# The end of the attention in a diffusion layer: one tile's output rows earlier, another's half moved, four roundings on another engine

## The chip, the cores and the metric

One NeuronCore of a Trainium2 chip runs one layer of a diffusion backbone. The metric is the device time of one execution in microseconds; smaller is better. Five engines work side by side, each through its own list of instructions in the order in which it was written, and they wait for each other by semaphores: PE (TensorE, matmuls), DVE (VectorE), ACT (ScalarE), POOL (GpSimd) and SP (SyncE, which issues the transfers).

## The reference

```python
def rmsnorm(x, g):
    xf = x.astype(jnp.float32)
    y = xf * lax.rsqrt(jnp.mean(xf * xf, axis=-1, keepdims=True) + EPS)
    return (y * g.astype(jnp.float32)).astype(x.dtype)
# window_attention: 8 query heads, 2 kv heads of 64; keys with |i-j| <= 128, 256 context keys, a sink logit
    p = jax.nn.softmax(jnp.concatenate([s_band, s_ctx, s_sink], axis=-1), axis=-1).astype(v.dtype)
    out = (jnp.einsum('bnhgqk,bnkhd->bnqhgd', p[..., :n_band], vb)
           + jnp.einsum('bnhgqc,bchd->bnqhgd', p[..., n_band:n_band + k_ctx.shape[1]], v_ctx))
def conv_glu(h, w_up, conv_w, conv_b, w_down):
    a, val = jnp.split(h @ w_up, 2, axis=-1)
    a = jax.nn.gelu(dwconv(a, conv_w, conv_b))
    return (a * val) @ w_down
```

The layer takes 1024 latent tokens of width 1024: the norm, an adaLN shift and scale, one input projection for an mLSTM group (4 heads of 128) and the window attention, both results side by side (512 + 512 columns) through one output projection `w_out`, gated and added to `x`; then the norm, shift and scale again and the ConvGLU (`D_FF` 2816), gated and added.

`rmsnorm(x)` is `x * rsqrt(mean(x * x) + EPS)`. All is float32 from outside.

## The kernel before

**Number format.** A float32 operand of a matmul is split into a rounded part (`hi`, written as `F32R`) and the rest (`lo = src - hi`), and a product is three matmuls: hi x hi, lo x hi, hi x lo (`mm3`, lines 305 to 307). The rounding is a copy with a change of type (CAST in the profile); it can be done on ACT or on DVE. The subtraction for `lo` is DVE's here (line 1210), and it reads what the rounding wrote.

**The window attention** goes over 32 pairs in stages `t` = 0 to 33, inside a `manual_schedule`: the code's order is each engine's order. In one stage the pair `N` starts, `A` has its scores and softmax, `C` transposes its probabilities (`tr`), splits them (`hi`, `lo`) and multiplies by the values (`pv`), and `E` finishes (`y1`, `y2` on DVE empty the product's bank `u`; its pool has one buffer). Between these steps stand slots: `fill(t, i)` runs what the dictionary `more[t, i]` holds. There the output projection of earlier tiles is spread: class `Wout` has `load` (the tile's rows `x2`), `hi` and `lo`, `mm(n, kt)` (one step of three matmuls; four steps make half `n` of a tile, 512 columns, in the bank `po`) and `add(n)` (DVE adds the bank to the rows; after `n` = 1 they are stored). `f0` is the attention part of tile 0; `tail_of(f0, n - 2)` puts its eight steps into stages 31, 32 and 33 (`n` = 32).

**The end of attention** is a loop over the other seven tiles in the order 4, 1, 5, 2, 6, 3, 7, inside a second `manual_schedule`. Iteration `i` with tile `b`: PE projects half 0 of the tile's attention rows (`wout_n(b, 0)`, 12 matmuls); ACT squares the second half of the tile before and takes the root (`sq(prev, 1)`); `norm_b(prev)` has DVE's reciprocal and ACT's scaling into `hn`; `evac(pp)` empties the transposes of the tile two before into `raw`, four pieces on ACT and four on DVE; DVE adds half 0 to the rows (`add0`); ACT squares it (`sq(b, 0)`); then the splits and sums that the FFN needs from tile `pp`; then PE projects half 1 (`wout_n(b, 1)`), transposes `prev` (`trans`), and DVE adds half 1 (`add1`). The projection banks of the loop, `pO2`, are two. `held` is a list of subtractions that `run` lets DVE do later.

In iterations 1, 3 and 5, `pp` is tile 0, 1 and 2, whose `raw` (128 x 1024) is split into the FFN's operand B11, with DVE for both parts; in iteration 0 DVE rounds `er`, a tile of FFN weights, into `e0`:

```python
V.tensor_copy(e0[0][:], er[:])
held.append(split(pp, B11, 2, raws[pp][:], V))
```

Ahead of the loop ACT squares tile 0's two halves into `hn` (`sq(0, 0)`, `sq(0, 1)`), takes the root (with a load of ACT's function table), and `norm_b(0)` follows. Behind the loop comes the FFN: long sequences of matmuls on `hB` (the split operands) and weights from `w_up`, then `w_down`. The FFN takes over half of the time.

Lines are those of the kernel before; the kernel after has the same code 27 to 29 lines further down.

Of the kernel before, what the change touches and what calls it, by code (L numbers as in the profile page):

```python
# [9 lines left out]
F32 = mybir.dt.float32  # L10
F32R = mybir.dt.float32r
BF16 = mybir.dt.bfloat16
AF = mybir.ActivationFunctionType
ALU = mybir.AluOpType
# [4 lines left out]
P = 128  # L19
D = 1024  # L20
# [14 lines left out]
EPS = 1e-6  # L35
BIG = 1e30
XW = 272
PB = 6
# [40 lines left out]
def build(tc, I, out, dbg=None):  # L79
    nc = tc.nc  # L80
    dbg = dbg or {}
    V, S, G, T = nc.vector, nc.scalar, nc.gpsimd, nc.tensor
# [13 lines left out]
    def spc(n, i=0, w=1):  # L96
        a = SP[n][0] + i
        return sp[:, a:a + w]
# [186 lines left out]
    hn = [0]  # L285
# [197 lines left out]
    m0, me = z, e_  # L483
    order = (list(range(NCH)), [1, 0] + list(range(NCH - 1, NC - 1, -1)))
# [450 lines left out]
    def load_q(b):  # L935
        QTs[b] = wm.tile([P, AH, P], F32R, name="QT", tag="QT", bufs=2)
        return nc.sync.dma_start(QTs[b][:].bitcast(F32), q_d[b]).ins
# [38 lines left out]
    n = 0  # L976
# [12 lines left out]
    for h in range(H):  # L989
# [3 lines left out]
        else:  # L993
# [12 lines left out]
            pq = rstk.enter_context(tc.tile_pool(name="pq", bufs=1, side="right"))  # L1006
# [60 lines left out]
    xs = {}  # L1067
# [140 lines left out]
    order = [4, 1, 5, 2, 6, 3, 7]  # L1208
    ys = {}
# [23 lines left out]
    more = collections.defaultdict(list)  # L1233
# [7 lines left out]
    def tail_of(w, t):  # L1241
        m = lambda n, k: lambda: w.mm(n, k)
        more[t + 1, 1] += [m(0, 0)]
        more[t + 1, 2] += [m(0, 1)]
        more[t + 2, 0] += [m(0, 2)]
        more[t + 2, 1] += [m(0, 3), lambda: w.add(0)]
        more[t + 3, 0] += [m(1, 0)]
        more[t + 3, 1] += [m(1, 1)]
        more[t + 3, 2] += [m(1, 2), m(1, 3), lambda: w.add(1)]

    def fill(t, i):
        for f_ in more.pop((t, i), ()):
            f_()

    w0, f0 = Wout(0, 0), Wout(0, 1)
# [4 lines left out]
    for b in range(1, NL):  # L1260
        token(Wout(b, 0), 4 * b - 2)
    n = len(pairs)
    more[n - 4, 0] += [f0.load]
    more[n - 3, 2] += [f0.hi, f0.lo]
    tail_of(f0, n - 2)
    more[n - 5, 0] += [lambda: ysplit_h(order[0], S)]
    more[n - 5, 2] += [lambda: ysplit_l(order[0])]
    more[n - 4, 0] += [lambda: ysplit_h(order[1], S)]
# [20 lines left out]
    for t in range(n + 2):  # L1289
        blk, nth = divmod(t, 4)  # L1290
        if nth == 0 and blk + 1 < NL:
            lq = load_q(blk + 1)
        if t in WOT:
            k = 4 + WOT.index(t)
            room = [wop.tile([P, D], F32R, name=f"wo{n}{k}")[:] for n in "hl"]
            with tc.issue_after(lq):
                wogs.append(load_wo(k, lambda room=room: room, G, True))
                next(wogs[-1])
        if t + 1 < len(pairs):
            live[t + 1] = Pair(*pairs[t + 1])  # L1300
        N, A, B, C, E = (live.get(t + 1 - i, null) for i in range(5))
        A.S(0)
        E.lo(2)
        B.nrm()
        fill(t, 3)
        rows_step()
        if t == 0:
            next(qpend.pop(0), 0)
            w0.tr()
            pdk.close()  # L1310
            pSs.append((pa_.enter_context(tc.tile_pool(name="pS", bufs=1, space=PSUM, side="right")), "s"))
            live[0].sk(1)
            w0.hi()
            live[0].S(1)
            w0.lo()
        E.pv(1)
        C.tr(0)
        E.pv(2)
        A.mxo(0)
        C.hi(0)  # L1320
        E.y1()
        A.ex(0)
        N.sk(0)
        C.lo(0)
        E.y2()
        fill(t, 0)
        if t == 0:
            for q in qpend:
                next(q, 0)
        C.tr(1)  # L1330
        if t:
            A.S(1)
        C.hi(1)
        A.mxo(1)
        fill(t, 1)
        C.tr(2)
        C.lo(1)
        A.ex(1)
        N.sk(1)
        C.hi(2)  # L1340
        fill(t, 2)
        C.pv(0)
        live.pop(t - 3, None)
# [19 lines left out]
    t5 = pb_.enter_context(tc.tile_pool(name="t5", bufs=2, reuse_waits="tile"))  # L1363
# [5 lines left out]
    B11, B21, B22, T1, T2, T3, T4 = range(7)  # L1369
# [5 lines left out]
    er = eW.tile([P, 2, 512], F32, name="er")  # L1375
    e0 = [eW.tile([P, 2, 512], F32R, name=f"e0{n}") for n in "hl"]
# [12 lines left out]
    hns, rs, pts, raws, tbs = ({} for _ in range(5))  # L1389
    last = order[-1]  # L1390

    def load_x(b):
        xs[b] = t3.tile([P, D], F32, name="x2", tag="x2")[:]
        nc.sync.dma_start(xs[b], x2_d[b][:])

    def wout_n(b, n, mid=None):
        ns = slice(512 * n, 512 * n + 512)
        po = pO.tile([P, 512], F32, name="po", tag="o")
        yh, yl = ys[b]
        for kt in range(4):  # L1400
            if kt == 3 and mid:
                mid()
            mm3(po[:], yh[:, kt], yl[:, kt], wos[4 + kt][0][:, ns], wos[4 + kt][1][:, ns], kt == 0, kt == 3)
        return lambda: V.tensor_tensor(out=xs[b][:, ns], in0=po[:], in1=xs[b][:, ns], op=ALU.add)
# [4 lines left out]
    def sq(b, n, mean=True):  # L1409
        if n == 0:  # L1410
            hns[b] = t5.tile([P, D], F32, name="hn", tag="hn")
            rs[b] = t5.tile([P, 3], F32, name="r2", tag="r2")
        ns = slice(512 * n, 512 * n + 512)
        S.activation(hns[b][:, ns], xs[b][:, ns], AF.Square, accum_out=rs[b][:, n:n + 1])
        if n == 1:
            if mean:
                run(1)
                mean0(b)
            S.activation(rs[b][:, 0:1], rs[b][:, 1:2], AF.Sqrt, bias=rs[b][:, 2:3], scale=1.0 / D)

    def norm_b(b, halves=False):
        run(1)
        V.reciprocal(rs[b][:, 0:1], rs[b][:, 0:1])
        if halves:
            S.activation(hns[b][:, 0:512], xs[b][:, 0:512], AF.Copy, scale=rs[b][:, 0:1])
            V.tensor_scalar(out=hns[b][:, 512:D], in0=xs[b][:, 512:D], scalar1=rs[b][:, 0:1], scalar2=None, op0=ALU.mult)
        else:
            S.activation(hns[b][:], xs[b], AF.Copy, scale=rs[b][:, 0:1])
# [26 lines left out]
    held = []  # L1455
# [5 lines left out]
    def split(b, blk, w, src, hi_eng=S):  # L1461
        ts = slice(b % 4 * P, b % 4 * P + P)
        hi, lo = (hB[i][:, blk:blk + w, :, ts] for i in range(2))
        (S.copy if hi_eng is S else hi_eng.tensor_copy)(hi, src)
        return lambda: sub(V, lo, src, hi.bitcast(F32))
# [28 lines left out]
                     skip_group_check=not first and len(kts) == 4)  # L1494

    add = lambda e, o, x, y: e.tensor_tensor(out=o, in0=x, in1=y, op=ALU.add)
    load_x(order[0])
    fence = tc.manual_schedule(engines={mybir.EngineType.PE, mybir.EngineType.DVE, mybir.EngineType.Activation,
                                        mybir.EngineType.Pool})
    fence.__enter__()  # L1500
    sq(0, 0)
    sq(0, 1)
    ys[order[2]] = [yh2[0], hB[1][:, T4, :, 3 * P:4 * P]]
    for j in range(3, 7):
        ysplit_h(order[j], G, [hB[n][:, B22 + j - 3, :, 3 * P:4 * P] for n in range(2)])
# [5 lines left out]
    for i, b in enumerate(order):  # L1511
        prev = order[i - 1] if i else None
        pp = order[i - 2] if i > 1 else 0 if i == 1 else None
        add0 = wout_n(b, 0)
        if prev is not None:
            sq(prev, 1)
            norm_b(prev)
        run()
        if pp is not None:
            evac(pp)  # L1520
        if i in (1, 2):
            ysplit_l(order[i + 4])
        if pp is not None and pp >= 4 and b != last:
            held.append(split_b(pp))
        add0()
        if i == 0:
            V.tensor_copy(e0[0][:], er[:])
            held += [lambda: None, lambda: sub(V, e0[1][:], er[:], e0[0][:].bitcast(F32))]
        sq(b, 0)
        if b == last:  # L1530
            break
        if pp is not None and pp < 4:
            held.append(split(pp, B11, 2, raws[pp][:], V))
            if late is not None:
                held.append(split_t3(late))
                held.append(split_t4(late))
            late = None
            run(1)
        if pp is not None and pp >= 4:
            sum1(pp)  # L1540
            sum2(pp)
            held.append(split_t1(pp))
            held.append(split_t2(pp))
            run(2)
            held += [lambda a=pp: sum3(a), lambda a=pp: sum4(a)]
            late = pp
        add1 = wout_n(b, 1)
        trans(prev if i else 0)
        add1()
        nc.sync.dma_start(x2_d[b][:], xs[b])  # L1550
        if i == 1:
            sub(V, r1[:, 1], er[:, 0], r1[:, 1])
        if i + 2 < len(order):
            load_x(order[i + 2])
# [50 lines left out]
    def wsplit_h(R, n):  # L1605
# [5 lines left out]
        def lo():  # L1611
# [42 lines left out]
                                                                    tag={"a": "a", "f": "b", "b": "b"}.get(n, "c"))  # L1654
# [219 lines left out]
    raws, ops = {}, {}  # L1874
# [77 lines left out]
    more = {}  # L1952
# [87 lines left out]
    for t, (p, ps, fresh) in enumerate(products):  # L2040
        for j in range(NP):
            n = NP * t + j
# [11 lines left out]
            if n - 1 in sums:  # L2054
                k = sums[n - 1]
                m = len(PAIRS[k])
                add(V, b11[k][:, 0:m], b22[k][:, 0:m], b11[k][:, 0:m])
            if n + 2 in raws:
                q, k = steps[n + 2]
# [10 lines left out]
            if n in sums:  # L2070
                k = sums[n]
# [5 lines left out]
            if NP + 3 <= n < NP + 3 + NL:  # L2077
                b = n - NP - 3
# [17 lines left out]
    n = len(steps) - 3  # L2096
# [100 lines left out]
```

## Time and profile before

| | |
|---|---|
| median of 3 runs | 1263.05 us (1262.92 to 1263.34) |
| the profiled execution | 1262.65 us, its span 1260.9 us |
| PE, DVE, ACT, POOL busy | 98%, 77%, 51%, 14% of the span |
| granted TensorE clock | 0.998 |
| stages 30 to 33 | about 557.2 to 576.2 us of the span |
| loop of the seven tiles | 576.2 to 628.9 us |
| FFN | from 628.9 us to the end |

All times inside the span are counted from its start. A row of the timeline gives start, duration, engine, line, operation and `out<-in`, then in brackets how long the engine stood idle before it and what released it. Matmuls are pipelined: one of 512 columns shows 0.39 us, but the next starts 0.23 us after it.

### The profile page before, as it was taken

The numbers are of one execution on the slowest core, as the hardware profiler recorded it, in microseconds if no ns is written. First come the engines' busy times: TensorE is split into PE (matmuls) and PEld (weight loads), VectorE is DVE, ScalarE is ACT, GpSimd is POOL, SyncE is SP. The second block draws the span as 40 slices with busy tenths as digits, with TensorE's granted clock in tenths as the row PEclk, the third lists the DMA queues.
The fourth block names the chain that finished last, engine by engine and source line by source line (L and its number), as shares of the span: only waits on it lengthen the run. The fifth ranks groups of instructions, "written<-read, shape, count | busy, mean of one in ns | idle before, by whom it ended". The sixth has DMA issues, their size and how long they took to land.

```text
span 1260.9 us, 19246 instructions
## 1 busy us (share of the span) xinstructions
PE 1234.0 (98%) x7044; PEld 1060.3 (84%) x7044; DVE 973.1 (77%) x1695; ACT 638.5 (51%) x1310; POOL 179.9 (14%) x158
## 2 busy tenths in 40 slices
PE   6999999999999999999999999999999999999997
PEld 4899999999898888888887888888888888888886
DVE  4863777777787888788987877777777777777887
ACT  6732556464865777776843333333333334434435
POOL 0200000000001443221002231232231230001000
PEclk9999999999999999999999999999999999999999
DMA  9541534362354333104313332233232238875563
GB/s 361 190 139 35 145 116 154 116 180 74 85 176 159 135 120 116 51 34 168 117 51 125 113 106 101 93 108 117 100 109 90 102 122 305 313 253 189 193 193 135
DMA packets 90560, 176.17 MB, mean 140 GB/s; under 512 B 12954, under 2 KB 29538, under 8 KB 90466
## 3 DMA queue, kind: packets, MB, share of 16 engines
q1 hardware_dynamic: 90178, 174.15, 41.0%
q8 instruction: 56, 0.92, 0.3%
q10 hardware_dynamic: 288, 0.79, 0.2%
q14 instruction: 38, 0.31, 0.1%
HBM read 136.58 MB, written 38.33 MB: 139 GB/s over the span
## 4 chain that ended last, share of the span: by engine, by line
PE 85%; DVE 6%; ACT 5%; DMA 2%; issue 2%; SPq 1%; ACTq 0%; DVEq 0%
PE pd L2034 16%; PE pc L1492 9%; PE pa L1492 9%; PE pp L600 7%; PE pe L1492 5%; PE pd L1492 4%; PE pb L1492 4%; PE u L1194 3%; PE pv L305 2%; PE pv L307 2%; PE pv L306 2%; PE pt L1171 2%; PE po L305 2%; PE po L307 1%; PE po L306 1%
## 5 line engine op out<-in xcount | busy, mean ns | idle before, releaser
L1609 ACT CAST wh<-Rb 128x1024 fp32r<-128x1024 f32 (+1 forms) x63 | 56.8, 903 | 144.4 <-PE pd L1492 77.4
L2034 PE MATMUL pd<-dh,ah 128*128 128x512 f32 x296 | 115.1, 389 | 0.0
L2034 PE MATMUL pd<-dl,ah 128*128 128x512 f32 x296 | 115.1, 389 | 0.0
L2034 PE MATMUL pd<-dh,al 128*128 128x512 f32 x296 | 115.1, 389 | 0.0
L1492 PE MATMUL pc<-hB,wh 128*128 128x512 f32 x344 | 105.6, 389 | 0.0
L1492 PE MATMUL pa<-hB,wh 128*128 128x512 f32 x336 | 103.7, 390 | 0.3 <-ACT sn L1691 0.2
L1210 DVE TENSOR_TENSOR wl<-Rb,wh 128x1024 fp32r<-128x1024 f32 (+1 forms) x63 | 65.7, 1045 | 39.1 <-ACT wh L1609 38.6
L600 PE MATMUL pp<-hl,wh 128*128 128x512 f32 x256 | 79.4, 405 | 0.0
L1728 POOL TENSOR_TENSOR tt<-vt,tt 128x512 f32<-128x512 f32 x21 | 27.3, 1301 | 353.4 <-ACT tt L1721 353.4
L1492 PEld LDWEIGHTS pc<-hB,wh 128*128 128x128 f32 x344 | 64.6, 188 | 13.4
L305 PE MATMUL pv<-wh,hl 128*128 128x256 f32 x256 | 75.9, 296 | 0.0
L1492 PEld LDWEIGHTS pa<-hB,wh 128*128 128x128 f32 x336 | 62.9, 188 | 14.2 <-ACT sn L1691 1.1
L307 PE MATMUL pv<-wh,hl 128*128 128x256 f32 x256 | 72.4, 283 | 0.0
L306 PE MATMUL pv<-wl,hl 128*128 128x256 f32 x256 | 72.3, 282 | 0.0
L1492 PE MATMUL pc<-hB,wl 128*128 128x512 f32 x172 | 66.4, 389 | 0.0
L1492 PE MATMUL pa<-hB,wl 128*128 128x512 f32 x168 | 65.4, 389 | 0.0
L2034 PEld LDWEIGHTS pd<-dh,al 128*128 128x128 f32 x296 | 55.6, 188 | 11.6
L2034 PEld LDWEIGHTS pd<-dh,ah 128*128 128x128 f32 x296 | 55.6, 188 | 11.5
L2034 PEld LDWEIGHTS pd<-dl,ah 128*128 128x128 f32 x296 | 55.6, 188 | 11.4
L1178 ACT CAST ph<-pt 128x512 fp32r<-128x512 f32 (+1 forms) x88 | 46.2, 525 | 25.9 <-PE pt L1171 25.7
L1148 DVE TENSOR_REDUCE nm<-sps 128x1 f32<-128x641 f32 (+1 forms) x64 | 50.2, 785 | 4.9 <-PE sps L1144 3.4
L1492 PE MATMUL pd<-hB,wh 128*128 128x512 f32 x176 | 54.0, 390 | 0.0
(1098 smaller groups left out, 3687.0 us busy)
## 6 DMA issues: line engine op xcount, KB each, us to landing
w<-in_w_ada_dram SPq DMA_DIRECT2D x64, 256.0 KB, 2.8
br<-in_w_down_dram SPq DMA_DIRECT2D x25, 512.0 KB, 5.1
ar<-act_s SPq DMA_DIRECT2D x44, 256.0 KB, 3.8
Ra<-in_w_up_dram SPq DMA_DIRECT2D x21, 512.0 KB, 3.6
Rb<-in_w_up_dram SPq DMA_DIRECT2D x21, 512.0 KB, 3.6
act_a<-tt SPq DMA_DIRECT2D x33, 256.0 KB, 2.0
act_s<-tt SPq DMA_DIRECT2D x33, 256.0 KB, 2.0
wr<-in_w_h_dram SPq DMA_DIRECT2D x16, 512.0 KB, 4.1
```

The lines of the kernel that those rows point to most:

```text
L305: T.matmul(ps, st_hi, mv_hi, start=first, stop=False)
L306: T.matmul(ps, st_hi, mv_lo, start=False, stop=False)
L307: T.matmul(ps, st_lo, mv_hi, start=False, stop=last)
L600: T.matmul(pp[:, 512 * n:512 * n + 512], wkq[sw][:, kt, cs], hl[n][part][:, kt, :], start=kt == 0 and sw + part == 0, stop=kt == KT - 1 an ...
L1148: V.tensor_reduce(out=self.nm[:, j:j + 1], in_=self.sv[j], axis=AX.X, op=ALU.max, negate=True)
L1178: S.copy(self.ph[i][:, :w], self.pt[i][:, :w])
L1194: T.matmul(self.u[:], vv[:, c, self.g], part[i][:, kk * 2 * P:(kk + 1) * 2 * P], start=kb + m == 0, stop=kb == last and m == 1)
L1210: sub = lambda e, o, x, y: e.tensor_tensor(out=o, in0=x, in1=y, op=ALU.subtract)
L1492: T.matmul(ps[:, cols], wt[sw][:, j, kt * P:kt * P + P], hB[part][:, blk, kt, cols], start=first and n == 0, stop=last and n == len(seq) - ...
L1609: S.copy(wt[0][:], src)
L1728: e.tensor_tensor(out=self.tt[:, h2_], in0=self.vt[:], in1=self.tt[:, h2_], op=ALU.mult)
L2034: T.matmul(ps[:], ac[sa][:, js], w[sw], start=first and n == 0, stop=last and n == 2, skip_group_check=not fresh)
```

## The change

It has four parts.

1. `f0`'s eight steps move one stage earlier, to stages 30, 31 and 32, its load two stages earlier. Its two `add`s go into a new slot 4, which stands behind `N.sk(0)` and ahead of `C.lo(0)`.
2. Half 0 of tile 4 (`f1`, 12 matmuls) moves out of the loop into stage 33, in the bank of `f0`; its x add comes behind the last `E.y2()`. The load of tile 4's rows moves to stage 28.
3. Tile 0's squares move into stage 32, its root with the table load into stage 33, its reciprocal behind the last `E.y2()`.
4. Four roundings of 128 x 1024 (e0, and B11 of tiles 0, 1 and 2) move from DVE to ACT.

```diff
-    more[n - 4, 0] += [f0.load]
+    f1 = Wout(order[0], 1)
+    r0 = spc("c", 4, 3)
+    def rows1():
+        f1.h, f1.l = (a.rearrange("p k t -> p (k t)") for a in ys[order[0]])
+    def sq0(h):
+        jk = pq.tile([P, 642], F32, name="p_", tag="p_", bufs=PB)[:, 0:256].bitcast(BF16)
+        S.activation(jk, xs[0][:, 512 * h:512 * h + 512], AF.Square, accum_out=r0[:, h:h + 1])
+        if h:
+            V.tensor_scalar(out=r0[:, 2:3], in0=r0[:, 0:1], scalar1=1.0 / D, scalar2=EPS, op0=ALU.mult, op1=ALU.add)
+    m0 = lambda n_, k: lambda: f0.mm(n_, k)
+    m1 = lambda k: lambda: f1.mm(0, k)
+    more[n - 6, 0] += [f0.load]
+    more[n - 4, 0] += [f1.load]
     more[n - 3, 2] += [f0.hi, f0.lo]
-    tail_of(f0, n - 2)
+    more[n - 2, 0] += [m0(0, 0)]
+    more[n - 2, 1] += [m0(0, 1)]
+    more[n - 2, 2] += [m0(0, 2)]
+    more[n - 1, 4] += [m0(0, 3), lambda: f0.add(0)]
+    more[n - 1, 1] += [m0(1, 0)]
+    more[n - 1, 2] += [m0(1, 1)]
+    more[n, 4] += [m0(1, 2), m0(1, 3), lambda: f0.add(1)]
+    more[n, 2] += [rows1, lambda: sq0(0), lambda: sq0(1)]
+    more[n + 1, 3] += [m1(0)]
+    more[n + 1, 0] += [m1(1)]
+    more[n + 1, 1] += [m1(2)]
+    more[n + 1, 2] += [m1(3), lambda: S.activation(r0[:, 0:1], r0[:, 1:2], AF.Sqrt, bias=r0[:, 2:3], scale=1.0 / D)]
+    more[n + 2, 0] += [lambda: V.reciprocal(r0[:, 0:1], r0[:, 0:1]), lambda: f1.add(0)]
...
         N.sk(0)
+        fill(t, 4)
         C.lo(0)
...
     def norm_b(b, halves=False):
         run(1)
-        V.reciprocal(rs[b][:, 0:1], rs[b][:, 0:1])
+        if b:
+            V.reciprocal(rs[b][:, 0:1], rs[b][:, 0:1])
...
-    load_x(order[0])
...
-    sq(0, 0)
-    sq(0, 1)
+    hns[0], rs[0] = t5.tile([P, D], F32, name="hn", tag="hn"), r0
...
-        add0 = wout_n(b, 0)
+        add0 = wout_n(b, 0) if i else lambda: None
...
-            V.tensor_copy(e0[0][:], er[:])
+            S.copy(e0[0][:], er[:])
...
-            held.append(split(pp, B11, 2, raws[pp][:], V))
+            held.append(split(pp, B11, 2, raws[pp][:]))
```

DVE in stage 32, before, from an FFN sum to the second `lo` (`pl__` is `lo` of the probabilities, `yT<-u,ut` are `y1` and `y2`, L1109 is `add(0)` of tile 0's rows):

```order
L1273 TENSOR_TENSOR yT<-ym 128x512
L1184 TENSOR_TENSOR pl__7378<-pt,ph 128x512
L1205 TENSOR_TENSOR yT<-u,ut 64x128
L1206 TENSOR_TENSOR yT<-u,ut 64x128
L1109 TENSOR_TENSOR x_7115<-po,x_7115 128x512
L1184 TENSOR_TENSOR pl__7396<-pt,ph 128x512
```

The same place after:

```order
L1300 TENSOR_TENSOR yT<-ym 128x512
L1109 TENSOR_TENSOR x_6955<-po,x_6955 128x512
L1184 TENSOR_TENSOR pl__7402<-pt,ph 128x512
L1205 TENSOR_TENSOR yT<-u,ut 64x128
L1206 TENSOR_TENSOR yT<-u,ut 64x128
L1184 TENSOR_TENSOR pl__7413<-pt,ph 128x512
```

The x add (now tile 0's second) has come ahead of `lo`, `y1` and `y2`.

ACT at the attention's end, before, from the last copies of `u` to the squares of tile 4 (x_7115 is tile 0, x_7502 tile 4):

```order
L1199 COPY ut<-u 64x128
L1200 COPY ut<-u 64x128
L1414 ACTIVATE hn,r_7507<-x_7115 128x512 x2
L1419 ACT_TABLE_LOAD
L1419 ACTIVATE r_7507<-r_7507 128x1
L1428 ACTIVATE hn<-x_7115,r_7507 128x1024
L1414 ACTIVATE hn,r_7539<-x_7502 128x512 x2
```

After (x_6955 is tile 0, x_7117 tile 4):

```order
L1291 ACT_TABLE_LOAD
L1291 ACTIVATE sp<-sp 128x1
L1199 COPY ut<-u 64x128
L1200 COPY ut<-u 64x128
L1457 ACTIVATE hn<-x_6955,sp 128x1024
L1554 CAST e0h<-er 128x1024
L1442 ACTIVATE hn,r_7540<-x_7117 128x512 x2
```

Table load and root stand ahead of the last copies, and the rounding of e0 between tile 0's `hn` and tile 4's squares.

DVE in iteration 3 (tile 2; `raw` is tile 1's), before, from `add0`:

```order
L1404 TENSOR_TENSOR x_7629<-po,x_7629 128x512
L1464 CAST hB_7482<-raw 128x8x128
L1210 TENSOR_TENSOR hB_7483<-raw,hB_7482 128x8x128
L1404 TENSOR_TENSOR x_7629<-po,x_7629 128x512
L1210 TENSOR_TENSOR hB_7483<-raw,hB_7482 128x4x128
L1407 TENSOR_SCALAR r_7730<-r_7730 128x1
```

And after, with ACT's rows of the same iteration behind DVE's:

```order
L1432 TENSOR_TENSOR x_7630<-po,x_7630 128x512
L1210 TENSOR_TENSOR hB_7506<-raw,hB_7505 128x8x128
L1432 TENSOR_TENSOR x_7630<-po,x_7630 128x512
L1210 TENSOR_TENSOR hB_7506<-raw,hB_7505 128x4x128
L1435 TENSOR_SCALAR r_7731<-r_7731 128x1
```

```order
L1480 ACTIVATE raw<-pt,ada_65 128x128 x4
L1442 ACTIVATE hn,r_7731<-x_7630 128x512
L1493 CAST hB_7505<-raw 128x8x128
L1493 CAST hB_7505<-raw 128x4x128 x2
L1442 ACTIVATE hn,r_7731<-x_7630 128x512
```

The rounding has left DVE's list, where the subtraction now follows `add0` directly, and stands on ACT behind the square of `add0`'s half.

## The prediction

> **What bounds the kernel now.** I read the page first, then busy time by stretch around the edited code, then the chain that ended last, then single instructions.
>
> ```profile
> span 1260.9 us, 19246 instructions
> PE 1234.0 (98%) x7044; PEld 1060.3 (84%) x7044; DVE 973.1 (77%) x1695; ACT 638.5 (51%) x1310; POOL 179.9 (14%) x158
> ```
>
> Over the whole span the matmul engine decides. The stretches say where that may be different: 557 to 576 us are the attention's stages 30 to 33, 576 to 629 the loop over the seven tiles, and then the FFN.
>
> ```profile
> core 0: us, PE busy (x) PEld busy (x) DVE busy (x) ACT busy (x) POOL busy (x), PEclk, DMA share, GB/s
> 557.20:566.50 9.30, 8.49 (x62) 7.46 (x61) 7.36 (x17) 6.95 (x19) 2.73 (x4) 1.00 0.14 56
> 566.50:576.20 9.70, 9.03 (x57) 7.44 (x56) 7.67 (x15) 4.17 (x10) 1.66 (x2) 1.00 0.23 67
> 600.90:613.50 12.60, 12.60 (x65) 10.65 (x64) 11.81 (x26) 9.88 (x23) 0.00 (x0) 1.00 0.44 158
> 613.50:628.90 15.40, 15.19 (x97) 13.76 (x96) 14.45 (x32) 13.67 (x32) 0.00 (x0) 1.00 0.29 103
> 628.90:1255.00 626.10, 624.19 (x2750) 515.49 (x2749) 491.21 (x555) 238.26 (x283) 103.31 (x66) 1.00 0.42 145
> ```
>
> PE idles 0.81 + 0.67 = 1.48 us in the last four stages, not at all in the middle of the loop and 0.21 us at its end; the FFN behind it is full on PE (624.19 of 626.10), so what is lost or won before 629 reaches the end whole. A full PE doesn't make the loop PE's alone: DVE is busy 11.81 of 12.60 us there, and the chain of waits leaves PE after tile 4's last product and is on DVE and ACT, the engines of all its longer pieces, from there to the last tile's norm:
>
> ```profile
> 581.68 0.24 PE po L307
> 581.94 0.69 DVE x L1404
> ...
> 623.76 0.48 DVE hn L1426
> ```
>
> That ladder (x add, squares, root, norm `hn`, transposes, evacuation, x add) hands each tile's `hn` to PE shortly before PE wants it. By the norm on ACT and the transposes on PE, for tiles 4 and 3, the second and the seventh of eight in line:
>
> ```profile
> 583.95 1.15 ACT L1428 ACTIVATE hn<-x,r 128x1024 f32<-128x1024 f32 x1 [0.23 <-DVE r L1423]
> 617.77 1.15 ACT L1428 ACTIVATE hn<-x,r 128x1024 f32<-128x1024 f32 x1 [0.29 <-DVE r L1423]
> 588.22 1.03 PE L1440 MATMUL pt<-ident,hn 128*128 128x128 f32 x8
> 619.21 0.60 PE L1440 MATMUL pt<-ident,hn 128*128 128x128 f32 x4
> ```
>
> The lead of `hn` over its transposes is 588.22 - 585.10 = 3.12 us at first and 619.21 - 618.92 = 0.29 in the end. The ladder is slower than PE already and has eaten nearly all its start. What lengthens it by more than 0.29 us shows on PE.
>
> **Part 1, the three B11 roundings (tiles 0, 1, 2) from DVE to ACT.** The second one, now, on DVE and then on ACT, with ACT's price for this shape last:
>
> ```profile
> 599.34 0.68 DVE L1404 TENSOR_TENSOR x<-po,x 128x512 f32<-128x512 f32 x1
> 600.17 0.69 DVE L1464 CAST hB<-raw 128x1024 fp32r<-128x1024 f32 x1
> 600.90 1.23 DVE L1210 TENSOR_TENSOR hB<-raw,hB 128x1024 fp32r<-128x1024 f32 x1
> 602.04 0.68 DVE L1404 TENSOR_TENSOR x<-po,x 128x512 f32<-128x512 f32 x1
> 600.05 0.63 ACT L1414 ACTIVATE hn<-x 128x512 f32<-128x512 f32 x1
> 600.68 1.12 ACT L1464 CAST hB<-raw 128x512 fp32r<-128x512 f32 x2
> 602.76 0.63 ACT L1414 ACTIVATE hn<-x 128x512 f32<-128x512 f32 x1 [0.95 <-DVE x L1404]
> 627.88 1.04 ACT L1609 CAST wh<-yT 128x1024 fp32r<-128x1024 f32 x1
> ```
>
> DVE saves a cast of 0.69, but its subtraction of the low part needs the rounded part, and on ACT the cast stands behind the tile's first Square, which itself waits for the add at 599.34. So the cast starts at 600.68, ends 1.04 later at 601.72, and the subtraction starts about 601.75 instead of 600.90. Behind it in DVE's order is the second x add (602.04, now 602.89), behind that ACT's second Square, the root, `hn` and the evacuations: **+0.85 us** on the ladder. The two small casts on ACT slide back by 1.04 into the 0.95 us that ACT idles, so they cost nothing more. At tile 3's first add (613.02) the same order stands, and I take **+0.85** again. At tile 1 the evacuation lasts longer than the add:
>
> ```profile
> 585.01 1.49 ACT L1451 ACTIVATE raw<-pt,ada 128x128 f32<-128x128 f32 x4
> 587.27 1.23 DVE L1210 TENSOR_TENSOR hB<-raw,hB 128x1024 fp32r<-128x1024 f32 x1
> ```
>
> ACT is free at 586.50; a Square (0.63 to the next start, as at 600.05) and the cast end at 588.17, so the subtraction starts 588.20, not 587.27: **+0.93**. In all 2.63 us on the ladder, less the 0.29 of lead left: **+2.34 at tile 3's transposes**. Nothing in the even iterations gives it back: there the order is unchanged and each link waits for the one before. Both ends: 3 x 1.04 + 0.08 = 3.2 if the small casts push too; and -0.2 (the hold of the last `hn`, below) if the casts cost no wait at all.
>
> The Trainium skill (Perfetto Trace Analysis, Optimizing Scalar/DVE Operations) says that ScalarE may take over work where DVE is saturated, and also that DVE is faster on what has a performance mode. The second half agrees with 0.69 against 1.04 above; the first would make this part a gain, which is rival A.
>
> **Part 2, tile 0's rows earlier (stages 30 to 32) and half of tile 4's in stage 33.** No matmul is added; what moves is PE's idle time. The instructions around its gaps, and then two pieces of the chain for the price of four transposes and of one matmul of a projection (a projection step is three, 0.69 us):
>
> ```profile
> 560.90 0.47 PE L1194 MATMUL u<-ph,vv 128*128 128x256 f32 x2 [0.55 <-ACT p__7268 L1152]
> 562.90 0.51 PE L1194 MATMUL u<-pl__7291,vv 128*128 128x256 f32 x2 [0.23 <-DVE pl__7291 L1184]
> 569.57 0.40 PE L307 MATMUL po<-woh,yml 128*128 128x512 f32 x1
> 570.12 0.48 PE L1194 MATMUL u<-ph,vv 128*128 128x256 f32 x2 [0.15 <-DVE yT L1206]
> 571.35 0.51 PE L1194 MATMUL u<-pl__7396,vv 128*128 128x256 f32 x2 [0.30 <-DVE pl__7396 L1184]
> 570.01 0.69 DVE L1109 TENSOR_TENSOR x<-po,x 128x512 f32<-128x512 f32 x1
> 570.62 0.68 DVE L1184 TENSOR_TENSOR pl__7396<-pt,ph 128x512 fp32r<-128x512 f32 x1
> 569.40 0.27 DVE L1205 TENSOR_TENSOR yT<-u,ut 64x128 f32<-64x128 f32 x1
> 575.11 0.39 PE L307 MATMUL po<-woh,yml 128*128 128x512 f32 x1
> 575.54 0.69 DVE L1109 TENSOR_TENSOR x<-po,x 128x512 f32<-128x512 f32 x1 [0.68 <-PE po L307]
> 571.86 0.44 PE pt L1171 x4
> 573.42 0.23 PE po L305
> ```
>
> Three steps in stage 30, 2.1 us, now stand ahead of the 0.55 and the 0.23: both close, -0.78. But in stage 32 DVE's order becomes x add, `lo`, y1, y2, where now the add comes behind y2, and the pair's first u product waits for that y2, since `pU` has one buffer. An add starts 0.43 us after its last matmul does (575.11 to 575.54), the next starts 0.61 later (570.62 - 570.01), and from a `lo` to the u product behind y2 it takes 0.61 to y1 and 0.72 on (569.40 to 570.12): 0.43 + 0.61 + 1.33 = 2.37 us after that matmul. (In stage 31 the add stands so too, but there PE has two more steps, 1.39 us, and the scores behind the transposes.) PE is there after the matmul and four transposes, 0.23 + 0.44 = 0.67, and so stalls 1.70 us (0.17 less in the measure of the brackets, which count from modelled ends: 0.15 where the starts say 0.32). The 0.15 and 0.30 go, since they were the add's. By the brackets 1.53 - 0.78 - 0.45 = +0.30; by starts, where the same five places give 0.67 + 0.16 + 0.39, 0.32 and 0.46, 1.70 - 1.22 - 0.78 = -0.30. I take **0**, with ends of -1.5 (all idle gone, no new stall) and +0.6.
>
> **Part 3, tile 0's squares and root into the stages, and the e0 copy to ACT.** Today squares, table load and root lie between ACT's last copy and `hn` of tile 0, under 24 matmuls. Now only the reciprocal and `hn` are left, but only 12 matmuls cover them, and the attention's last product comes 12 x 0.23 = 2.8 us later. `hn` of tile 0 then starts about where it does now. Behind it ACT has the e0 copy (1.04) ahead of tile 4's two Squares, of which the second must follow tile 4's last add. If PE gains nothing in part 2, they end up to 0.66 us late (1.04 less the 0.3 to 0.4 us that ACT waits there now); if PE is 0.6 ahead, not at all. I take **+0.1**. DVE's own saved 0.68 us is worth nothing here: its next x add waits for PE.
>
> Removing tile 4's late load is free: PE reaches those rows only in stage 33, and the load is now issued four stages before the attention's last.
>
> **Late next:** the last `hn` (tile 7) holds PE today and still does:
>
> ```profile
> 624.30 0.66 PE L1440 MATMUL pt<-ident,hn 128*128 128x128 f32 x4 [0.21 <-DVE hn L1426]
> ```
>
> Sum: 2.34 + 0 + 0.1 = **+2.45 us**. The profiled execution took 1262.65 (span 1260.9 and 1.75 around it), 0.40 below the median of 1263.05, so 1265.10 there and **1265.5** as a median. 0.2% is 2.53 us, about what a measurement of this kernel can tell from no change, so the forecast sits just inside that bound, at 1265.58.
>
> **Rivals.**
>
> A. The roundings are free on ACT, because its 0.95 us of idle time per odd tile takes them: the ladder then is 0.7 us shorter three times and PE alone bounds the loop. For it: ACT is busy 9.88 of 12.60 us. Against it: that idle time comes after the cast is needed, not before. It decides if the cast starts before the Square, at the end of ACT's evacuation. Price: 0 + 0.1 - 0.21 gives 1262.9, not slower. By the first half of the skill's rule it would come out so.
>
> B. The stall of stage 32 doesn't arise, because y2 needs not follow the add by as much as I sum: PE and the whole ladder behind it start 1.70 us earlier, 1265.5 - 1.7 = 1263.8. For it: the transposes before it depend on ACT and may be late themselves. Against it: DVE runs in written order, and the add can't start before its matmuls end.
>
> C. ACT becomes the ladder: the e0 copy costs its 0.66 whole, part 2 its +0.6: 1265.5 + 0.56 + 0.6 = 1266.7. For it: `hn` of tile 0 has lost half its cover. Against it: both are upper ends at once of things that offset each other.
>
> **How the numbers follow.** My forecast has 0.53 (1264.6 to 1266.2), A 0.16, B 0.16, C 0.15. The range 1262.4 to 1266.9 leaves out a part of A and of C. Slower by over 0.2%: C and half of the forecast, 0.42; faster: only A and B together, 0.05; within: 0.53.
>
> **What would show it.** Right: a PE wait of about 1.5 us on `yT` in stage 32 and none on `p__` in 30; DVE's subtraction of B11 starting about 2.4 us after each odd tile's first add instead of 1.56, with ACT's cast as its releaser; PE waits for `x` or `hn` from tile 2's transposes on, 2 us and more in all; the FFN unchanged but shifted. Wrong: no PE wait between 600 and 620, or the subtraction starting no later than now, which would be A; or the waits there with the end unmoved, which would mean that the FFN had room that its 624.19 of 626.10 us doesn't show.

## The result

The kernel after takes 1265.99 us (median of 13 runs, 1264.84 to 1266.94), that before 1263.19 (13 runs, 1262.75 to 1264.01): +2.8 us, ratio 1.0024 with a 95% interval of 1.0017 to 1.0031. It is slower, clear of 1; whether by more than the 0.2% that the prediction used as a bound stays open, since the interval holds 1.0020. The forecast was +2.45.

The page of after first, then busy time by stretch (the columns are those of before; the loop now ends at 631.1):

```profile
span 1263.1 us, 19247 instructions
PE 1233.6 (98%) x7044; PEld 1059.5 (84%) x7044; DVE 970.1 (77%) x1691; ACT 641.7 (51%) x1314; POOL 180.0 (14%) x158
```

```profile
557.20:566.50 9.30, 9.30 (x63) 8.22 (x63) 7.04 (x16) 6.29 (x17) 2.73 (x4) 1.00 0.14 56
566.50:576.20 9.70, 7.96 (x50) 6.72 (x49) 6.84 (x15) 5.44 (x15) 1.65 (x2) 1.00 0.25 81
600.90:613.50 12.60, 11.60 (x54) 8.99 (x54) 10.47 (x23) 9.98 (x22) 0.00 (x0) 1.00 0.45 162
613.50:631.40 17.90, 16.85 (x102) 14.37 (x101) 15.42 (x35) 15.91 (x37) 0.00 (x0) 1.00 0.23 89
```

PE does the same work (1233.6 us), and its idle time has moved. The first stretch (stage 30 and most of 31) has none now, the second has 1.74 us, and the second half of the loop, which had 0.21 us in all, has 1.00 + 1.05. What PE waited for, first in the stages, then in the loop (us in all, number of waits, the longest in us):

```profile
PE u L1194 <- DVE yT L1206: 1.5, 1, 1.5
PE u L1194 <- DVE pl__7364 L1184: 0.2, 1, 0.2
```

```profile
PE po L305 <- DVE x L1432: 1.5, 3, 0.5
PE pt L1469 <- DVE hn L1455: 0.4, 1, 0.4
PE pt L1469 <- ACT hn L1457: 0.2, 1, 0.2
```

Two executions can't be laid over each other by their own clocks here: the loads and the projections ahead of the change took 0.78 us less in the profiled execution of after. So I count from PE's first score matmul of stage 30. Here that row and the first FFN matmul into `pf`, of before and then of after:

```profile
557.24 0.28 PE L1137 MATMUL sps<-kT,QT 128*128 128x256 f32 x1
628.91 0.45 PE L1492 MATMUL pf<-hB,wh 128*128 128x512 f32 x1
```

```profile
556.46 0.28 PE L1137 MATMUL sps<-kT,QT 128*128 128x256 f32 x1
631.10 0.45 PE L1521 MATMUL pf<-hB,wh 128*128 128x512 f32 x1
```

From stage 30 to the FFN it takes 71.67 us before and 74.64 after: +2.97, of the size of the +2.80 in the times. From `pf` to the span's end it is 632.0 us in both, so the FFN carries the loss unchanged.

The second rounding in after, DVE's rows and then ACT's:

```profile
599.85 0.68 DVE L1432 TENSOR_TENSOR x<-po,x 128x512 f32<-128x512 f32 x1
602.25 1.23 DVE L1210 TENSOR_TENSOR hB<-raw,hB 128x1024 fp32r<-128x1024 f32 x1 [1.73 <-ACT hB L1493]
603.40 0.68 DVE L1432 TENSOR_TENSOR x<-po,x 128x512 f32<-128x512 f32 x1
600.56 0.63 ACT L1442 ACTIVATE hn<-x 128x512 f32<-128x512 f32 x1
601.19 2.08 ACT L1493 CAST hB<-raw 128x1024 fp32r<-128x1024 f32 x3
604.11 0.63 ACT L1442 ACTIVATE hn<-x 128x512 f32<-128x512 f32 x1 [0.85 <-DVE x L1432]
```

The subtraction starts 2.40 us after the first x add instead of 1.56: DVE stands 1.73 us for ACT's cast, and the second x add follows 3.55 us after the first instead of 2.70. That is 0.85 more, and the two others show the same 1.73. `hn` of tiles 4, 1, 2 and 3, after:

```profile
583.61 1.16 ACT L1457 ACTIVATE hn<-x,r 128x1024 f32<-128x1024 f32 x1 [0.23 <-DVE r L1452]
590.93 1.15 ACT L1457 ACTIVATE hn<-x,r 128x1024 f32<-128x1024 f32 x1 [0.23 <-DVE r L1452]
605.45 1.15 ACT L1457 ACTIVATE hn<-x,r 128x1024 f32<-128x1024 f32 x1 [0.29 <-DVE r L1452]
619.97 1.15 ACT L1457 ACTIVATE hn<-x,r 128x1024 f32<-128x1024 f32 x1 [0.28 <-DVE r L1452]
```

Counted from stage 30 (27.15, 34.47, 48.99, 63.51 us; before 26.71, 33.18, 46.86, 60.53) they come later by 0.44, 1.29, 2.13 and 2.98: a start of 0.44 and then three steps of 0.85.

### The profile page after: what moved, and what is told of

Its sections match the earlier page's. It is cut to its first block, busy times and chain, and to the rows that moved or that the text cites. A ratio compares the mean times of both kernels' runs of the same rounds, so it can differ in the third digit from the quotient of the medians.

```text
span 1263.1 us, 19247 instructions
## 1 busy us (share of the span) xinstructions
PE 1233.6 (98%) x7044; PEld 1059.5 (84%) x7044; DVE 970.1 (77%) x1691; ACT 641.7 (51%) x1314; POOL 180.0 (14%) x158
## 4 chain that ended last, share of the span: by engine, by line
PE 84%; DVE 6%; ACT 4%; DMA 3%; issue 2%; SPq 1%; ACTq 0%; DVEq 0%
PE pd L2061 16%; PE pc L1521 9%; PE pa L1521 9%; PE pp L600 7%; PE pe L1521 5%; PE pd L1521 4%; PE pb L1521 4%; PE u L1194 3%; PE pv L305 2%; PE pv L307 2%; PE pv L306 2%; DMA wa<-in_w_ada_dram 2%; PE pt L1171 2%; DVE hB L1210 1%; PE po L305 1%
```

## The experiments

Each row counts from stage 30 as above. "hn 4" and "hn 3" are the starts of the norms of tile 4 and tile 3 on ACT, the second and the seventh of the eight; in before they are 26.71 and 60.53, the FFN's start 71.67. The last column is the FFN's start less that of before.

The trace columns come from one execution each. The times of most pairs of neighbours (after and e4, after and e5, e1 and e6) have intervals that overlap, so steps of about a microsecond rest on the trace, where the same step taken from two kernels agrees to 0.25 us: B11 on ACT costs 2.44 (e1), 2.69 (e2), 2.63 (e5 less e6) and 2.54 (e4 less e9).

| kernel | median, us | before beside it | ratio (95%) | hn 4 | hn 3 | FFN's start | against before |
|---|---|---|---|---|---|---|---|
| after | 1265.99 | 1263.19 | 1.0024 (1.0017 to 1.0031) | 27.15 | 63.51 | 74.64 | +2.97 |
| e1: after, B11 on DVE | 1263.30 | 1262.95 | 1.0002 (0.9993 to 1.0010) | 27.21 | 61.05 | 72.20 | +0.53 |
| e2: before, B11 on ACT | 1265.92 | 1262.95 | 1.0022 (1.0013 to 1.0031) | 26.73 | 63.21 | 74.36 | +2.69 |
| e3: after, cast before Square | 1264.07 | 1262.95 | 1.0009 (1.0000 to 1.0018) | 27.14 | 62.01 | 73.14 | +1.47 |
| e4: after, e0 on DVE | 1266.26 | 1262.95 | 1.0027 (1.0017 to 1.0037) | 27.79 | 64.13 | 75.27 | +3.60 |
| e5: after, add behind y2 | 1265.08 | 1263.04 | 1.0015 (1.0006 to 1.0024) | 25.99 | 62.37 | 73.51 | +1.84 |
| e6: e1 and e5 | 1262.57 | 1263.04 | 0.9996 (0.9987 to 1.0005) | 25.96 | 59.74 | 70.88 | -0.79 |
| e7: e6, two subtractions on POOL | 1263.77 | 1263.04 | 1.0003 (0.9995 to 1.0012) | 26.78 | 60.56 | 71.69 | +0.02 |
| e8: after, the same on POOL | 1266.87 | 1263.04 | 1.0030 (1.0019 to 1.0042) | 27.95 | 64.30 | 75.44 | +3.77 |
| e9: after, all four on DVE | 1263.97 | 1262.62 | 1.0010 (1.0001 to 1.0018) | 27.78 | 61.58 | 72.73 | +1.06 |
| e10: e6, DVE's list cleared | 1262.35 | 1262.62 | 0.9997 (0.9988 to 1.0006) | 24.92 | 59.43 | 70.57 | -1.10 |
| e12: the same again | 1261.91 | 1262.92 | 0.9992 (0.9983 to 1.0001) | 24.91 | 59.40 | 70.53 | -1.14 |
| e11: e10, mean first | 1261.70 | 1262.92 | 0.9991 (0.9982 to 1.0000) | 24.92 | 58.90 | 70.04 | -1.63 |

**e1, the three roundings back on DVE.**

```diff
-            held.append(split(pp, B11, 2, raws[pp][:]))
+            held.append(split(pp, B11, 2, raws[pp][:], V))
```

> The kernel after with only the three B11 roundings back on DVE. Theory (the ladder): each rounding on ACT lengthens the chain of DVE and ACT by 0.85 us; without them 2.5 us come back, about 1263.5 us, DVE's subtraction follows the tile's first add by 1.56 us again, and PE waits for no x add in the loop. Rival (the stall of 1.5 us in stage 32 and the later products are what costs): the time stays at 1266.0, since that stall is still there.

2.44 us of the 2.97 come back, and PE waits for no x add in the loop, though the stall in stage 32 is still there:

```profile
PE u L1194 <- DVE yT L1206: 1.5, 1, 1.5
PE u L1194 <- DVE pl__7364 L1184: 0.2, 1, 0.2
```

**e2, the kernel before with only those three on ACT.**

```diff
-            held.append(split(pp, B11, 2, raws[pp][:], V))
+            held.append(split(pp, B11, 2, raws[pp][:]))
```

> The kernel before with only the three B11 roundings moved to ACT. Ladder: 3 x 0.85 less the 0.29 us of lead at tile 3's transposes, +2.3, about 1265.5 us, with PE waits on x adds or hn from tile 2 on. Rival (stage 32's stall): 1263.2, no change, since stages 30 to 33 are those of before.

+2.69 by the trace and about +3.0 in time: one edit of one line makes nearly the whole loss, and the waits of PE in the loop are those of after:

```profile
PE po L305 <- DVE x L1404: 1.0, 2, 0.6
PE pt L1440 <- DVE hn L1426: 0.4, 1, 0.4
PE pt L1440 <- ACT hn L1428: 0.2, 1, 0.2
```

**e3, the cast ahead of the Square.** The same instructions on the same engines, two of them exchanged on ACT:

```diff
-        sq(b, 0)
-        if b == last:
-            break
         if pp is not None and pp < 4:
             held.append(split(pp, B11, 2, raws[pp][:]))
+        sq(b, 0)
+        if b == last:
+            break
+        if pp is not None and pp < 4:
```

> The kernel after with ACT's B11 rounding ahead of the Square of the tile's first half, the same work on each engine. Ladder by order: the rounding starts when ACT's evacuation ends, so DVE's subtraction comes 0.6 us sooner each time (still about 0.25 later than with DVE's own rounding): -1.8 us, about 1264.2. Rival (ACT is simply too loaded, or its slower cast is the price): each subtraction waits as long as now or only a little less, 1265.7 to 1266.0.

```profile
600.49 0.69 DVE L1432 TENSOR_TENSOR x<-po,x 128x512 f32<-128x512 f32 x1
602.40 1.23 DVE L1210 TENSOR_TENSOR hB<-raw,hB 128x1024 fp32r<-128x1024 f32 x1 [1.22 <-ACT hB L1493]
601.32 1.05 ACT L1493 CAST hB<-raw 128x1024 fp32r<-128x1024 f32 x1
```

DVE waits 1.22 instead of 1.73 us; the FFN starts 1.50 us sooner than in after (1.8 was expected), 0.50 for each rounding. ACT's load is the same, so that 0.50 of each 0.85 is the order on ACT. The other 0.35 is about what ACT's slower cast takes, 1.05 us to DVE's 0.69: the cast starts when ACT's evacuation ends, as DVE's did in before (600.17, behind an evacuation from 598.65 that lasted 1.49).

**e4, only e0 back on DVE.**

```diff
-            S.copy(e0[0][:], er[:])
+            V.tensor_copy(e0[0][:], er[:])
```

> The kernel after with only the e0 rounding back on DVE. Ladder: tile 4's squares come earlier on ACT, hn of tile 4 up to 0.4 us sooner by the trace counted from stage 30, and with it everything behind: 1265.5. Rival (the copy is hidden under tile 4's last products): hn of tile 4 at the same place, 1266.0. The two are told apart by the trace more than by the time.

A miss, and neither theory: `hn` of tile 4 comes 0.64 us *later* than in after. By the trace the move of e0 to ACT is a gain, here and between e9 and e1 (0.53); the times are too close to tell. It also shows where the start of the chain is set, in DVE's list between tile 4's two x adds, of after:

```profile
579.27 0.69 DVE L1109 TENSOR_TENSOR x<-po,x 128x512 f32<-128x512 f32 x1
579.88 1.81 DVE L1210 TENSOR_TENSOR hB<-yT,hB 128x512 fp32r<-128x512 f32 x2
581.62 0.68 DVE L1432 TENSOR_TENSOR x<-po,x 128x512 f32<-128x512 f32 x1
```

The second add waits for nothing that the trace shows: it stands behind two `hB` subtractions, which before ran ahead of the first add, under tile 4's 24 matmuls. In e4 DVE's cast of e0 stands there too.

**e5, the x add of stage 32 behind y2.**

```diff
-    more[n, 4] += [m0(1, 2), m0(1, 3), lambda: f0.add(1)]
+    more[n, 4] += [m0(1, 2), m0(1, 3)]
+    more[n, 0] += [lambda: f0.add(1)]
```

> The kernel after with one thing moved: in stage 32 the x add of tile 0's second half stands behind y2 again. Theory (DVE's order makes the stall): PE's 1.53 us wait for yT goes, and since PE and the chain of DVE and ACT both start at the attention's last product, all behind it comes 1.5 us sooner: about 1264.5 us. Rival (the chain at the loop's start is bound by DVE's backlog of subtractions, not by PE): tile 0's transposes come sooner, hn of tile 3 doesn't, 1266.0.

The wait for `yT` falls from 1.5 to 0.2 us, and `hn` of tile 4 and the FFN come 1.16 and 1.13 us sooner than in after, where 1.5 was expected. The stall was DVE's order, and the chain did not hide it: the chain's own start moved with it.

**e6, e1 and e5 together.** The two edits above.

> The last two cures together: the three B11 roundings on DVE, and the x add behind y2. If both costs are separate, 1263.3 - 1.5 = 1261.8 us, faster than before. Rival (the chain is bound elsewhere once one of them is gone): 1263.0 or more.

By the trace -0.79, 1.32 less than e1. In time the interval holds 1, so faster isn't shown. The sum was 0.8 us too hopeful in time: transposes of tile 0 start 1.72 us sooner than before, but `hn` of tile 4 only 0.75, and `hn` of tile 3 and the FFN 0.79: the chain bounds the loop's end.

**e7 and e8, two subtractions on POOL.** On e6, and on after:

```diff
-    for j in range(2, 5):
-        ysplit_l(order[j])
+    ysplit_l(order[2])
+    for j in range(3, 5):
+        sub(G, ys[order[j]][1], yslice(order[j]), ys[order[j]][0].bitcast(F32))
```

> As the kernel with both cures, and two of the three subtractions for hB (tiles 2 and 6), which DVE does between tile 4's two x adds, moved to POOL. Theory (DVE's backlog holds back tile 4's second add by about 1 us): hn of tile 4 comes about 0.5 us sooner counted from stage 30, then tile 3's transposes no longer wait for hn, 0.5 to 0.8 less: about 1261.2. Rival (ACT, with the e0 copy ahead of tile 4's squares, sets hn of tile 4): no change, 1261.8.

> The kernel after with only those two subtractions moved to POOL. Backlog theory: hn of tile 4 0.5 us sooner and everything behind with it, since the chain bounds the loop here: 1265.5. ACT theory: unchanged, 1266.0. The trace, counted from stage 30, decides between them.

Both start the FFN later than the kernels they are made from, by 0.81 and 0.80 us. The subtraction of e0 in after, and then e8, DVE and POOL:

```profile
582.28 1.21 DVE L1210 TENSOR_TENSOR e0l<-er,e0h 128x1024 fp32r<-128x1024 f32 x1
```

```profile
581.25 0.69 DVE L1432 TENSOR_TENSOR x<-po,x 128x512 f32<-128x512 f32 x1 [0.58 <-PE po L307]
582.73 0.15 DVE L1435 TENSOR_SCALAR r<-r 128x1 f32<-128x1 f32 x1 [0.79 <-ACT hn L1442]
582.80 2.19 DVE L1210 TENSOR_TENSOR e0l<-er,e0h 128x1024 fp32r<-128x1024 f32 x1
```

```profile
581.37 2.54 POOL L1210 TENSOR_TENSOR hB<-yT,hB 128x512 fp32r<-128x512 f32 x2
```

Tile 4's second add now waits only for PE, as meant. But e0's subtraction, 1.21 us in after, takes 2.19 beside POOL's, and `hn` is behind it. DVE's mean waits 0.79 us for ACT's first Square, which stands behind the e0 copy: with the add out of the way, that copy is next in line, so the prediction's worry about it was only one place too early.

**e9, all four roundings on DVE.** The edits of e1 and e4.

> The kernel after with all four roundings back on DVE: the moved projections, squares and root alone. If the costs add (three B11 roundings 2.4, e0 on DVE 0.6 dearer than on ACT): 1263.2 + 0.35 + 0.6 = 1264.2 us, slower than before though tile 0's transposes start 0.5 us sooner. Rival (what is left of the change is free without the roundings): 1263.0 or less.

+1.06 by the trace, near the sum of 0.53 (e1) and 0.64 (e4), and the interval is clear of 1: the moved rows, squares and root alone cost time, though tile 0's transposes start 0.5 us sooner than before.

**e10 and e12, DVE's list cleared.** On e6; `e0l(j)` is half `j` of the e0 subtraction:

```diff
-    for j in range(2, 5):
-        ysplit_l(order[j])
+    ysplit_l(order[2])
+    e0l = lambda j: sub(V, e0[1][:, j], er[:, j], e0[0][:, j].bitcast(F32))
...
-            S.copy(e0[0][:], er[:])
-            held += [lambda: None, lambda: sub(V, e0[1][:], er[:], e0[0][:].bitcast(F32))]
+            held += [lambda: None, lambda: ysplit_l(order[3])]
         sq(b, 0)
+        if i == 1:
+            S.copy(e0[0][:], er[:])
+        if i == 4:
+            e0l(0)
...
             sub(V, r1[:, 1], er[:, 0], r1[:, 1])
+            ysplit_l(order[4])
...
+    e0l(1)
     evac(prev)
```

> As the kernel with both cures (B11 on DVE, x add behind y2), and DVE's work between tile 4's x adds taken out: the two hB subtractions go behind tile 4's mean and behind tile 1's second x add, the e0 rounding on ACT behind tile 1's first square, the e0 subtraction in two halves into idle time of DVE in iterations 4 and 6. Theory (DVE's backlog there sets the start of the chain): hn of tile 4 about 1.3 us sooner counted from stage 30, no PE wait before the last tile's hn, about 1261.5 us. Rival (tile 1's rows, which are loaded only after tile 0's hn is done, hold the chain next): half of it, 1262.2.

> The kernel e10_ladder_start once more, beside the last one on the same chip. Its trace, counted from stage 30, put the FFN's start 1.1 us sooner than before; theory: 1.0 us under before in time as well, if the loads ahead of stage 30 don't differ. Rival: no difference from before, which would mean that the time ahead of stage 30 pays for it.

`hn` of tile 4 comes 1.04 us sooner than in e6 (1.3 was expected), so what DVE and ACT did ahead of tile 4's second add and its Squares held it; the two subtractions and the two steps of e0 moved together here, and the run doesn't say how much each held. The FFN starts only 0.3 us sooner: the added subtraction in iteration 1 takes 0.7 of it back (`hn` of tile 1 follows tile 4's by 7.15 us instead of 6.45, and ACT's root waits 0.60 us for DVE's mean), and PE's lead is used up again at tile 3. In time -0.3 and -1.0 us; each interval alone reaches 1.

**e11, the mean ahead of those subtractions.**

```diff
-            sub(V, r1[:, 1], er[:, 0], r1[:, 1])
-            ysplit_l(order[4])
+            held += [lambda: None, lambda: (sub(V, r1[:, 1], er[:, 0], r1[:, 1]), ysplit_l(order[4]))]
```

> As the kernel before this one (both cures, DVE's work taken out from between tile 4's x adds), and in iteration 1 DVE's mean ahead of the two subtractions on which ACT's root waited 0.60 us. Theory (the chain still bounds PE at tile 3's transposes): hn of tile 1 about 0.45 us sooner, PE's gap at tile 3's transposes (0.25) gone, about 0.3 us less: 1262.0 beside 1262.6 of before. Rival (PE alone bounds the loop by now): hn sooner, the end unmoved.

`hn` of tile 1 comes 0.51 us sooner than in e10 and the FFN 0.53; 0.45 and 0.3 were expected. By the trace it is the best of all, -1.63, and -1.2 in time, the interval just reaching 1.0000. What is left of PE's waits from stage 32 on:

```profile
PE pt L1470 <- DVE hn L1456: 0.3, 1, 0.3
PE u L1194 <- DVE yT L1206: 0.2, 1, 0.2
```

So with the rows moved and DVE's list put in order the trace gains 1.6 us on before. How much of that the moved rows bring isn't shown: the kernel before with only its lists put in order was not run.

## Why the prediction came out

**Part 1, the roundings: right, by its own steps, but for the lead.** Forecast: 0.93, 0.85 and 0.85 on the chain. Measured: 0.85 three times, with the cast in its forecast place behind the Square (in e2, on the kernel before, 0.93, 0.86 and 0.87); e2 makes most of the loss with this part alone, e1 takes it away, e3 takes 1.50 of it back by order alone. The signs named ahead came too: DVE's subtraction 2.40 us behind the first add with ACT's cast as its releaser, and 2.1 us of PE waits for `x` and `hn`. What was wrong is the 0.29 us of lead that the forecast took off. It was read at tile 3's transposes, but the last `hn` already held PE by 0.21 us in before, so at the last hand-over there was no lead: `hn` of tile 7 comes 2.96 us later than before, and the FFN 2.97.

**Part 2, the moved rows: the mechanism right, the size inside its ends of -1.5 and +0.6.** The stall for `yT` was forecast at 1.53 us in the brackets' measure and is 1.53:

```profile
572.00 0.47 PE L1194 MATMUL u<-ph,vv 128*128 128x256 f32 x2 [1.53 <-DVE yT L1206]
```

The gaps of 0.55 and 0.23 closed. I took 0 between +0.30 and -0.30; tile 0's transposes start 0.53 us sooner counted from stage 30, beyond the lower of the two, so the count by starts was the better one. This gain of PE's did not reach the end, because the chain started later.

**Part 3, the copy of e0: the wrong reason.** I put +0.1, with up to 0.66 us for ACT's copy ahead of tile 4's squares, and called DVE's saved 0.68 worthless since its next add waits for PE. The chain starts 0.44 us late, but because DVE's next add waits for DVE: the change puts tile 4's first add right behind the attention's last `y2`, which itself comes 2.15 us later counted from stage 30, and two subtractions that had run ahead of that add now stand between tile 4's adds. ACT idles 0.34 us ahead of the second Square, so the copy costs nothing there, and on DVE it would cost 0.64. The step that failed is the one that read DVE's order around the move without asking what else lands in the gap.

**The rivals.** A (the roundings are free on ACT) fell with e2: ACT idles 0.85 us there too, behind the cast, where it is of no use. The rule of the Trainium skill (Perfetto Trace Analysis, Optimizing Scalar/DVE Operations) that ScalarE may relieve a saturated DVE was satisfied in its condition, DVE being busy 11.81 of 12.60 us, and it didn't help, because DVE needed the result next. By the trace it did help for e0, whose rounding ends at 581.37 us on ACT while DVE's next add starts at 581.62 and the subtraction that reads it at 582.28. B (no stall in stage 32) fell with the row above. C fell in both halves, ACT's copy with e4 and part 2's 0.6 with the 0.53 that tile 0's transposes gain, though the time lies between my forecast and it.

The sum by the measured terms: 0.44 + 3 x 0.85 = 2.99, beside 2.98 at `hn` of tile 3, 2.97 at the FFN and 2.80 in time. The direction and the range held; the forecast's own figure was 0.35 us low in time, by the lead that it took off and the start that it put at +0.1.

The table says more than the prediction did. In every kernel the FFN's start and `hn` of tile 3 differ from before by the same amount to 0.01 us, from -1.63 to +3.77, and PE waits for the last `hn` in all of them, before too (0.21 to 0.41 us). So the chain (x add, Squares, norm, transposes, evacuation), and not PE's own list of products, sets the loop's end, although PE is 98% busy over the span. A gain of PE's counts only as far as it starts the chain sooner: in e1 tile 0's transposes start 0.48 us sooner than before and the FFN 0.53 later.

## What to carry to other kernels

Moving an operation to a less busy engine helped here only where nobody on the busy engine waited for it soon: ask where it stands in the new engine's list and who reads it next, not how much idle time that engine has. An engine that is 98% busy can still be fed by a slower chain: compare, tile by tile, when the chain delivers and when the bound engine takes, and read the lead at the last hand-over, not at one before it. When work is moved in one engine's list, read what ends up between two links of the chain on every other engine's list, and see in the order itself which waits now stand ahead of a buffer that PE needs.

## What the runs showed of the hardware that I had not expected

POOL and DVE slowed each other: a subtraction of 128 x 1024 on DVE took 2.19 us beside one on POOL, in both kernels that had it, and 1.21 without. In after the two `hB` subtractions between tile 4's adds took 1.81 us together beside POOL's four casts, which took 3.18; in e10, where these subtractions come behind the casts, they took 0.68 each and the casts 2.72. So the backlog at the chain's start was itself stretched by POOL. The Trainium skill (Perfetto Trace Analysis, Optimizing Scalar/DVE Operations) says that GPSIMD and DVE share an SBUF read port, so that moving work between them might not help, and the rows agree; that the port is the cause was not tried apart.

The stretch ahead of stage 30, the same code but for earlier loads, ended between 556.46 and 559.39 us in the profiled executions shown here. That spread is as large as the effect, and is why changes of a microsecond were read from a fixed row in the trace. Trace and median time agree to about 0.4 us, but for e7 (+0.02 and +0.73) and e10 (-1.10 and -0.27).
